# PE in source order through eight stages of a two-model kernel, with three head steps ahead of the second transposes

## The chip, the cores and the metric

The kernel runs on one core of one Trainium2 chip. The metric is the device time of one execution in microseconds; the time before is the median of three runs. The engines are called PE (TensorE, matrix products and transposes), DVE (VectorE), ACT (ScalarE), POOL (GpSimd) and SP (SyncE, which here only issues DMAs).

## The reference

256 tokens of width 1024 pass through two small models, one after the other, all in float32. What is computed, cut to the order of the parts:

```python
# first model
h = x + 0.5 * rmsnorm(swiglu(rmsnorm(h, g0), w_gu, w_down), g1)     # layer 0, FFN f00
h = h + rmsnorm(short_gated_conv(rmsnorm(h, g2)), g3)               # conv
h = h + 0.5 * rmsnorm(swiglu(rmsnorm(h, g4), ...), g5)              # FFN f01
k, v = split(rmsnorm(h, kv_norm_g) @ w_kv)                          # shared keys and values
h = h + 0.5 * rmsnorm(swiglu(rmsnorm(h, g0), ...), g1)              # layer 1, FFN f10
h = h + rmsnorm(diff_attention(rmsnorm(h, g2), k, v, ...), g3)
h = h + 0.5 * rmsnorm(swiglu(rmsnorm(h, g4), ...), g5)              # FFN f11
# second model
x = h
x = x + retention(rms_norm(x, mix_norm[0]), ...)
x = x + swiglu_2(rms_norm(x, ffn_norm[0]), ...)                     # FFN f20
x = x + stick_breaking(rms_norm(x, mix_norm[1]), ...)
x = x + swiglu_2(rms_norm(x, ffn_norm[1]), ...)                     # FFN f21
```

`swiglu` is `(silu(gate) * up) @ w_down` with a hidden width of 2816; a normed update divides the result of a stage by its root mean square before it is added to `h`.

## The kernel before

**Stages.** The kernel is a chain of stages, each a large projection from `h`, some work in the middle, and a projection back into two accumulators `acc0` and `acc1` (one for each half of 128 tokens). Stage 0 is f00, 1 conv, 2 f01, 3 the keys (`kproj`) with f10 behind them, 4 attention, 5 f11, 6 retention, 7 f20, 8 stick breaking, 9 f21. Each stage has *heads* (the first steps of its projection, for half A and for half B), a *body*, and *tails* (the steps that project back into `acc`).

**Weights.** The weights come in 280 units of 1 MB in a fixed order (`plan`). `W.load` starts the DMA of the next unit into one of three `raw` buffers; `W.split` lets ACT cast a unit into a high part `whi` (L171) and DVE subtract to get a low part `wlo` (L172), so that a product is made of three matmuls (`mm3`: L274, L275, L276; `mm_row`: L297, L300, L303). There are five slots for split units and a few spare places. `W.pump(n)` splits up to n more units as far as there is room.

**Boundary.** Between two stages, `boundary` interleaves the tails of the old stage with the heads of the new one. The tails of half A come first. `chain_A[0]` updates `h` of half A from `acc0` (squares on ACT at L386 and L388, products on DVE at L387 and L389, a power on POOL at L392, the update of `h` at L394; for a plain sum only L376 on DVE). `chain_A[1]` is eight transposes of `h` on PE (`tr_x`, L338), whose results ACT and DVE scale and split into `xT` (L321, L323); the square of `h` (L347) follows. Then come the last tail of half B, `chain_B[0]`, the first n head steps of half A, and `chain_B[1]`, the transposes of half B. A head step is twelve matmuls. In `kproj`, attention and retention the third head step also ends with four transposes of a finished column (`tr`, `tr_q`, `rotate`). Transposes write into two PSUM buffers (`ps_tr`), or, while the list `borrowed` holds a half, into that half's accumulator.

**Order on the engines.** The program is written in one sequence; a scheduling layer then picks the order of each engine's instructions by the readiness that it expects, with the source as the priority. Inside `tc.manual_schedule(engines={...})` the named engines keep the order of the source. The kernel before does that for ACT in stages 8 and 9, and for all engines in the first weight splits of the opening.

**Opening of f00.** `start` loads `x` transposed in pieces beside the first two weight units, then `h`, then the third unit. Its first two units are used by `by_tile` (48 matmuls), then come two steps of `gu(1, ...)` of 24 matmuls each, the transposes of the hidden tiles (`tr`, L520), `across` (which spreads `rstd` over the partitions by DVE at L358 and two products on PE at L359), and from column 2 on `whole` (32 matmuls each, L487 and L490). `dn` multiplies by the down projection into `acc`.

**Attention.** `s1` to `s3` make scores and their softmax, `pv1` transposes the weights of the heads (`aA`, `aB`) and copies them out, `pv2` multiplies by `v` and starts a chain over ACT, DVE and POOL (square, sum, power, product `yo` at L888), and `tr_o` transposes `yo` into the input `xk` of the projection back. In the tails `out(j, half)` is twelve matmuls.

Of the kernel before, what the change touches and what calls it, by code (L numbers as in the profile page):

```python
# [194 lines left out]
def tile_two_models(ctx: ExitStack, tc: tile.TileContext, a: dict):  # L195
# [66 lines left out]
    borrowed = []  # L262
# [139 lines left out]

    def boundary(prev_tail, chain_A, chain_B, head_A, head_B, few):
        for s in prev_tail[0]:
            s()
            W.pump(1)
        chain_A[0]()
        for s in prev_tail[1][:2]:  # L410
            s()
        chain_A[1]()
        if few:
            W.pump(1)
        for s in prev_tail[1][2:]:
            s()
        chain_B[0]()
        W.pump(1)
        n = 3 if few == 2 else 2
        for s in head_A[:n]:  # L420
            s()
        chain_B[1]()
        W.pump(1)
        for s in head_A[n:]:
            s()
            W.pump(1)
        for s in head_B:
            s()
            W.pump(1)

    def ffn(tag, xT, rstd, skew=True, first=None, last_stage=False, opening=False):
# [7 lines left out]
        def gu(c, half, j, last=True):  # L439
            if j == 0:  # L440
                gu_ps[c, half] = new_mm()
            mm_col(gu_ps[c, half], xT[half], (tag, "gu", c), j, last)
            if j == 1:
                evict(c, half)
# [69 lines left out]
        def tr(c, half):  # L514
            if c not in hT:
                hT[c] = k4.tile([P, 2, 2, 2, P], F32R, tag="k4", name=f"hT{c}")
            t = new_tr("tr_h")
            src = hid.pop((c, half))
            for k in range(2):
                T.transpose(t[:, k * P : k * P + P], src[:, k * P : k * P + P], ident)  # L520
            split_plain(t[:, 0:256].rearrange("p (k t) -> p k t", k=2), hT[c][:, half, 0], hT[c][:, half, 1])
# [22 lines left out]
        def body():  # L544
            nonlocal first
            if opening:
                for j in range(2):
                    by_tile(0, j)
                    W.pump()
                for j in range(2):  # L550
                    for half in range(2):
                        gu(1, half, j, last=half == 1)
                    W.pump()
                    for half in range(2):
                        borrowed.append(half)
                        if j == 0:
                            tr(0, half)
                        elif half == 0:
                            across(rstd)
                            acc.update(factors(rstd))  # L560
                        borrowed.pop()
            for c in range(2 if skew or opening else 0, NCH):
                for j in range(2):
                    whole(c, j)
                    borrowed.append(0)
                    if first is not None:
                        first()
                        first = None
                    if opening and c == 2 and j == 0:
                        tr(1, 0)  # L570
                        borrowed[-1] = 1
                        tr(1, 1)
                    if skew and c == 2 and j == 0:
                        tr(1, 1)
                    borrowed[-1] = 1
                    if not opening and c == (2 if skew else 0) and j == 0:
                        across(rstd)
                        acc.update(factors(rstd))
                    borrowed.pop()
                    W.pump()  # L580
                if 2 <= c < NCH - 1:
                    for half in range(2):
                        dn(c - 2, half, last=half == 1)
                    W.pump()
# [754 lines left out]
    def start(make, gcols):  # L1339
        xT, rstd = {}, {}  # L1340
        stage = make(xT, rstd)
        x_t = [k4.tile([P, 4, 2, P], F32, tag="k4", name=f"x_t{g}") for g in range(2)]

        def x_load(k, n):
            Q.dma_start(x_t[k // 4][:, k % 4 : k % 4 + n], a["x_t"][:, k : k + n])

        with tc.manual_schedule(engines={mybir.EngineType.Activation}):
            S.dma_start(gains, a["gains"])
            S.activation(small(tag="t"), nhalf[:, 0:1], AF.Silu)
        ones = junk(512)  # L1350
        V.memset(ones, 1.0)
        warm = new_acc(0, "warm")[:, 0:512]
        for _ in range(WARM):
            T.matmul(warm, ones[:, 0:P], ones, start=True, stop=True)
        W.load(4, lambda p: p % 2 or x_load(p, 2))
        x_load(4, 2)
        W.load(2, lambda p: p and x_load(6, 2))
        for half in range(2):
            Q.dma_start(h[half], x[0, half * P : half * P + P])
        W.load()  # L1360
        for half in range(2):
            xT[half] = new_xT(half)
        hi, lo = (xts[-1][:, i] for i in range(2))

        def x_in(k):
            src = x_t[k // 4][:, k % 4]
            S.activation(hi[:, k], src, AF.Copy, scale=gcols[:, k : k + 1])
            V.scalar_tensor_tensor(
                lo[:, k], src, gcols[:, k : k + 1], hi[:, k].bitcast(F32), ALU.mult, ALU.subtract
            )  # L1370

        with tc.manual_schedule():
            W.split(4, lambda p: x_in(p))
            W.split(4, lambda p: x_in(4 + p))
            for half in range(2):
                rstd[half] = rms_of(half)
        return stage

    def stage(n, make, update, gcols, prev, spares=(), gb=None, few=0, end=None):

        xT, rstd = {}, {}
        ch = xchain(update, prev[1], gcols, xT, rstd)
        heads, body, tails, acc = make(xT, rstd)
        W.spares = list(spares)
        boundary(prev[0], ch[0], ch[1], heads[0], heads[1], few)
        W.spares = []
        if end is not None:
            end()
        if gb is not None:
            gbs.append(load_gb(*gb))  # L1390
        body()
        return tails, acc
# [3 lines left out]
    def mk_ffn(tag, **kw):  # L1396
        return lambda xT, rstd: ffn(tag, xT, rstd, **kw)
# [11 lines left out]
        Q.dma_start(out[0, P : 2 * P], h[1])  # L1409

    TWO = [(0, 1), (2, 3)]
    heads, body, tails, acc = start(mk_ffn("f00", skew=False, opening=True), g_norm(0, 0))
    gbs.append(load_gb(0, 1))
    body()
# [14 lines left out]
    kT = big(2, [P, 8, 2 * P], F32, "kT")  # L1429
    heads, tr_k = kproj(xk, rstd_k, kT)  # L1430
    W.spares = [(3, 4)]
    boundary(cur[0], ch[0], ch[1], heads[0], heads[1], 0)
    W.spares = []
    gbs.append(load_gb(1, 1))
    heads, body, tails, acc = ffn("f10", xT, rstd_k, skew=False, first=lambda: tr_k(1, 1))
# [4 lines left out]
    cur = stage(5, mk_ffn("f11"), add_normed(gbs[-1], 1.0), g_norm(1, 4), cur, [(2, 3)], gb=(1, 5), few=1)  # L1440
    cur = stage(6, retention, add_normed(gbs[-1], HALF), g_cols(G_MIX, 8), cur, TWO)
    cur = stage(7, mk_ffn("f20"), add_plain, g_cols(G_FFN, 8), cur, TWO)
    act_order = tc.manual_schedule(engines={mybir.EngineType.Activation})
    act_order.__enter__()
    cur = stage(8, stick, add_plain, g_cols(G_MIX + 8, 8), cur, TWO)
# [60 lines left out]
```

## Time and profile before

| what | value |
|---|---|
| median of 3 runs (lowest to highest) | 1597.99 us (1597.76 to 1599.32) |
| the profiled execution's own time | 1596.82 us |
| span of its profile | 1595.0 us |
| PE busy | 1570.0 us, 98% |
| DVE busy | 1088.0 us, 68% |
| ACT busy | 926.8 us, 58% |
| POOL busy | 61.2 us, 4% |
| mean granted TensorE clock | 0.998 of full speed |
| DMA | 300.94 MB, 189 GB/s on average |

The span is what the profile sees from the first to the last instruction; 1.8 us of the execution lie outside it. PE is busy almost all of the time, and a busy matmul overlaps the next one, so what is lost on PE is read from the starts of its instructions.

### The profile page before, as it was taken

The page shows a single profiled execution, that of the slowest core. Times are in us where ns is not written, and L with a number is a line of the kernel's source. Part 1 is how long each engine was busy: PE and PEld are TensorE (multiplying, and loading weights), DVE is VectorE, ACT ScalarE, POOL GpSimd, SP SyncE. Part 2 cuts the span into 40 slices and gives each one's busy share as a digit, 9 for nine tenths or more (in the row PEclk, how much of TensorE's full clock was granted, in tenths as well). Part 3 has the DMA queues.
Part 4 walks back from the last instruction along what each step waited for, and adds up shares of the span by engine and source line. Part 5 has one row for each costly group of instructions (what it writes and reads, how often), then busy time and mean ns, then how long its engine had stood idle before and what let it go on. Part 6 is the DMA issues. An engine that isn't in the chain of part 4 may idle for free.

```text
span 1595.0 us, 21678 instructions
## 1 busy us (share of the span) xinstructions
PE 1570.0 (98%) x8395; PEld 1374.9 (86%) x8395; DVE 1088.0 (68%) x1742; ACT 926.8 (58%) x1611; POOL 61.2 (4%) x65
## 2 busy tenths in 40 slices
PE   8999999999999999989999999999999999999998
PEld 6899888899989999877899888888899988688997
DVE  6766867666677666787666776456567666666664
ACT  6655656555676555676555554556455566655552
POOL 0000100000000000001000010000000021000000
PEclk9999999999999999999999999999999999999999
DMA  8655644555545555444455555545455553235551
GB/s 331 238 211 189 247 159 175 204 203 197 211 175 205 205 196 213 148 159 163 176 202 209 203 196 185 185 158 188 164 206 203 205 205 138 101 134 210 211 193 46
DMA packets 43448, 300.94 MB, mean 189 GB/s; under 512 B 4864, under 2 KB 4992, under 8 KB 8016
## 3 DMA queue, kind: packets, MB, share of 16 engines
q1 hardware_dynamic: 42768, 297.81, 51.6%
q0 software_dynamic: 432, 1.64, 0.3%
q8 instruction: 66, 1.08, 0.3%
q14 instruction: 38, 0.31, 0.1%
q10 hardware_dynamic: 144, 0.09, 0.0%
HBM read 298.48 MB, written 1.05 MB: 188 GB/s over the span
## 4 chain that ended last, share of the span: by engine, by line
PE 86%; DVE 6%; ACT 4%; issue 1%; POOL 1%; DMA 1%; ACTq 0%; POOLq 0%
PE mm L487 24%; PE mm L490 12%; PE acc L303 8%; PE acc L297 8%; PE acc L300 8%; PE mm L276 7%; PE mm L274 7%; PE mm L275 7%; DVE wlo L172 2%; ACT whi L171 1%; PE tr L632 1%; POOL r L392 1%; PE tr_x L338 1%; DMA raw<-in_w 1%; PE z L1246 1%
## 5 line engine op out<-in xcount | busy, mean ns | idle before, releaser
L172 DVE TENSOR_TENSOR wlo<-raw,whi 128x1024 fp32r<-128x1024 f32 (+1 forms) x536 | 636.1, 1214 | 319.4 <-ACT whi L171 318.7
L171 ACT CAST whi<-raw 128x1024 fp32r<-128x1024 f32 (+1 forms) x536 | 540.4, 1045 | 332.3 <-issue 134.3
L487 PE MATMUL mm<-xT,whi 128*128 128x512 f32 x1792 | 584.0, 382 | 0.0
L490 PE MATMUL mm<-xT,wlo 128*128 128x256 f32 x1792 | 453.2, 273 | 0.0
L487 PEld LDWEIGHTS mm<-xT,whi 128*128 128x128 f32 x1792 | 326.3, 190 | 36.5
L490 PEld LDWEIGHTS mm<-xT,wlo 128*128 128x128 f32 x1792 | 342.7, 191 | 11.8
L274 PE MATMUL mm<-whi,xT 128*128 128x512 f32 x488 | 191.1, 392 | 2.0 <-ACT whi L171 1.4
L275 PE MATMUL mm<-wlo,xT 128*128 128x512 f32 x488 | 185.6, 380 | 0.7 <-DVE wlo L172 0.6
L276 PE MATMUL mm<-whi,xT 128*128 128x512 f32 x488 | 185.5, 380 | 0.0
L297 PE MATMUL acc<-whi,hT 128*128 128x512 f32 x516 | 153.9, 380 | 0.0
L303 PE MATMUL acc<-whi,hT 128*128 128x512 f32 x516 | 153.8, 379 | 0.0
L300 PE MATMUL acc<-wlo,hT 128*128 128x512 f32 x516 | 153.5, 379 | 0.0
L300 PEld LDWEIGHTS acc<-wlo,hT 128*128 128x128 f32 x516 | 97.5, 189 | 13.9
L303 PEld LDWEIGHTS acc<-whi,hT 128*128 128x128 f32 x516 | 97.5, 189 | 13.8
L297 PEld LDWEIGHTS acc<-whi,hT 128*128 128x128 f32 x516 | 97.3, 189 | 12.3 <-DVE hT L330 0.2
L274 PEld LDWEIGHTS mm<-whi,xT 128*128 128x128 f32 x488 | 92.1, 189 | 17.8 <-issue 2.3
L275 PEld LDWEIGHTS mm<-wlo,xT 128*128 128x128 f32 x488 | 92.3, 189 | 14.8 <-DVE wlo L172 2.3
L276 PEld LDWEIGHTS mm<-whi,xT 128*128 128x128 f32 x488 | 92.2, 189 | 14.2 <-DVE xT L323 1.2
L503 ACT COPY part<-mm 128x256 f32<-128x256 f32 x112 | 41.5, 371 | 55.6 <-PE mm L487 55.6
L329 ACT CAST hT<-hid 128x256 fp32r<-128x256 f32 x112 | 45.4, 405 | 26.1 <-DVE hid L511 26.1
L511 DVE TENSOR_TENSOR hid<-gated,sg 128x256 f32<-128x256 f32 x112 | 47.6, 425 | 11.8 <-ACT sg L507 3.7
L508 ACT COPY part<-mm 128x256 f32<-128x256 f32 x112 | 41.7, 372 | 19.1 <-PE mm L487 19.1
(246 smaller groups left out, 1622.6 us busy)
## 6 DMA issues: line engine op xcount, KB each, us to landing
raw<-in_w SPq DMA_DIRECT2D x276, 1024.0 KB, 4.8
gb<-in_norm_g SPq DMA_DIRECT2D x6, 512.0 KB, 5.6
x_t<-in_x_t SPq DMA_DIRECT2D x4, 256.0 KB, 5.5
raw<-in_w SPq DMA_DIRECT2D x4, 256.0 KB, 4.6
raw<-in_w SPq DMA_DIRECT2D x2, 512.0 KB, 7.0
h<-in_x SPq DMA_DIRECT2D x2, 512.0 KB, 8.4
dec<-in_decay POOLq DMA_DIRECT2D x1, 768.0 KB, 9.3
out<-h SPq DMA_DIRECT2D x1, 512.0 KB, 4.6
```

The source lines that it names most:

```text
L171: self.nc.scalar.copy(hi[:, c], raw[:, c])
L172: self.nc.vector.tensor_tensor(lo[:, c], raw[:, c], hi[:, c].bitcast(F32), ALU.subtract)
L274: T.matmul(o, xh, wh, start=start, stop=False)
L275: T.matmul(o, xh, wl, start=False, stop=False)
L276: T.matmul(o, xl, wh, start=False, stop=stop)
L297: T.matmul(acc[:, n * 512 : n * 512 + 512], xh(kts + k), columns(wh, c), start=st, stop=False)
L300: T.matmul(acc[:, n * 512 : n * 512 + 512], xh(kts + k), columns(wl, c), start=False, stop=False)
L303: T.matmul(acc[:, n * 512 : n * 512 + 512], xl(kts + k), columns(wh, c), start=False, stop=sp[n])
L329: S.copy(hi, tr)
L487: T.matmul(ps[n], wh[:, w], x2, start=kk == 0, stop=kk == 7, skip_group_check=True)
L490: T.matmul(o, wl[:, w], x2[:, 0], start=False, stop=False, skip_group_check=True)
L511: V.tensor_tensor(hd, t[1], sg, ALU.mult)
```

## The change

The order of PE is fixed to the source from the opening to the end of the body of stage 7. `boundary` takes the number of head steps of half A that run ahead of half B's transposes as an argument: three for a normed update (before, three only at the boundary into attention and two elsewhere), two for a plain one. In the opening, the third weight unit is loaded ahead of `h` and split in the manually ordered region ahead of the squares of `h`; the transposes of the hidden tile of column 0 follow the second step of column 1, one behind each half; `across` moves behind the first `whole` of column 2; the two transposes of column 1 follow the two `whole` steps of column 2, one each, both into `acc0`.

```diff
-    def boundary(prev_tail, chain_A, chain_B, head_A, head_B, few):
+    def boundary(prev_tail, chain_A, chain_B, head_A, head_B, few, ahead):
...
-        n = 3 if few == 2 else 2
-        for s in head_A[:n]:
+        for s in head_A[:ahead]:
             s()
         chain_B[1]()
         W.pump(1)
-        for s in head_A[n:]:
+        for s in head_A[ahead:]:
...
                         gu(1, half, j, last=half == 1)
+                        if j == 1:
+                            borrowed.append(half)
+                            tr(0, half)
+                            borrowed.pop()
                     W.pump()
-                    for half in range(2):
-                        borrowed.append(half)
-                        if j == 0:
-                            tr(0, half)
-                        elif half == 0:
-                            across(rstd)
-                            acc.update(factors(rstd))
-                        borrowed.pop()
...
-                    if opening and c == 2 and j == 0:
-                        tr(1, 0)
-                        borrowed[-1] = 1
-                        tr(1, 1)
+                    if opening and c == 2:
+                        tr(1, j)
...
-                    if not opening and c == (2 if skew else 0) and j == 0:
+                    if c == (2 if skew or opening else 0) and j == 0:
                         across(rstd)
...
+        W.load()
         for half in range(2):
             Q.dma_start(h[half], x[0, half * P : half * P + P])
-        W.load()
...
             W.split(4, lambda p: x_in(4 + p))
+            W.split()
             for half in range(2):
                 rstd[half] = rms_of(half)
...
-        boundary(prev[0], ch[0], ch[1], heads[0], heads[1], few)
+        boundary(prev[0], ch[0], ch[1], heads[0], heads[1], few, 2 if update is add_plain else 3)
...
+    pe_order = tc.manual_schedule(engines={mybir.EngineType.PE})
+    pe_order.__enter__()
     heads, body, tails, acc = start(mk_ffn("f00", skew=False, opening=True), g_norm(0, 0))
...
-    boundary(cur[0], ch[0], ch[1], heads[0], heads[1], 0)
+    boundary(cur[0], ch[0], ch[1], heads[0], heads[1], 0, 3)
...
     cur = stage(7, mk_ffn("f20"), add_plain, g_cols(G_FFN, 8), cur, TWO)
+    pe_order.__exit__(None, None, None)
```

## Rows read from the trace of the kernel before

**Rows 1.** The page's busy times: engine, busy us, share, instructions.

```profile
PE 1570.0 (98%) x8395; PEld 1374.9 (86%) x8395; DVE 1088.0 (68%) x1742; ACT 926.8 (58%) x1611; POOL 61.2 (4%) x65
```

**Rows 2.** PE's timeline in the opening: start, us, instruction, [idle before <-releaser].

```profile
17.04 0.38 PE L276 MATMUL mm<-whi,xT 128*128 128x512 f32 x1
...
20.42 0.70 PE L274 MATMUL mm<-whi,xT 128*128 128x512 f32 x2 [1.41 <-ACT whi L171]
...
22.00 0.38 PE L276 MATMUL mm<-whi,xT 128*128 128x512 f32 x1
22.22 0.38 PE L274 MATMUL mm<-whi,xT 128*128 128x512 f32 x1
```

**Rows 3.** DMA in the opening: SP's timeline, landing of issues 5 to 8 us, a window.

```profile
7.84 7.87 SPq L149 DMA_DIRECT2D raw<-in_w  x3
...
raw<-in_w SPq DMA_DIRECT2D x1, 1024.0 KB, 10.1
...
8.00:14.00 6.00, 5.97 (x27) 4.53 (x26) 4.51 (x9) 5.00 (x11) 0.00 (x0) 1.00 1.04 411
```

**Rows 4.** ACT's and DVE's timelines in the opening.

```profile
18.40 0.37 ACT L329 CAST hT<-tr_h 128x256 fp32r<-128x256 f32 x1 [0.34 <-PE tr_h L520]
...
19.32 5.79 ACT L171 CAST whi<-raw 128x1024 fp32r<-128x1024 f32 x6
...
18.80 0.42 DVE L330 TENSOR_TENSOR hT<-tr_h,hT 128x256 fp32r<-128x256 f32 x1 [0.29 <-ACT hT L329]
...
40.29 0.23 DVE L358 COPY spread<-rstd 128x128 f32<-128x128 f32 x1 [0.77 <-PE tr_r L359]
```

**Rows 5.** Windows, head matmuls alone: stretch, its us, PE busy (count), clock, DMA.

```profile
185.10:193.90 8.80, 7.32 (x32) 1.00 0.69 248
275.10:283.00 7.90, 6.64 (x30) 1.00 0.84 293
452.20:463.10 10.90, 9.64 (x43) 1.00 0.66 231
746.50:752.50 6.00, 5.34 (x24) 1.00 0.70 258
924.30:932.50 8.20, 7.87 (x34) 1.00 0.58 182
651.10:662.30 11.20, 8.82 (x38) 1.00 0.76 260
```

**Rows 6.** Windows, matmuls into the accumulators alone, same columns.

```profile
906.10:922.30 16.20, 15.49 (x71) 1.00 0.71 255
732.90:738.10 5.20, 4.35 (x19) 1.00 0.00 0
```

**Rows 7.** PE's timeline at transposes that wait, boundaries and attention.

```profile
662.36 0.66 PE L338 MATMUL tr_x<-ident,h 128*128 128x128 f32 x4 [1.29 <-ACT qT L798]
...
708.89 1.09 PE L632 MATMUL tr<-ident,yo 128*128 128x128 f32 x4 [3.54 <-DVE r L883]
...
724.17 0.70 PE L297 MATMUL acc<-whi,xk 128*128 128x512 f32 x2 [1.05 <-ACT xk L897]
...
738.17 0.66 PE L632 MATMUL tr<-ident,yo 128*128 128x128 f32 x4 [0.92 <-DVE yo L888]
...
922.34 1.29 PE L338 MATMUL tr_x<-ident,h 128*128 128x128 f32 x8 [0.66 <-DVE h L394]
...
924.40 0.48 PE L274 MATMUL mm<-whi,xT 128*128 128x512 f32 x1 [0.56 <-ACT xT L321]
```

**Rows 8.** A window behind the longest wait: all engines' busy times, then clock, DMA.

```profile
708.90:712.20 3.30, 3.30 (x11) 2.85 (x12) 1.87 (x6) 1.99 (x8) 0.00 (x0) 0.50 0.38 161
```

**Rows 9.** POOL's and DVE's timelines at the first boundary.

```profile
179.97 0.55 POOL L392 TENSOR_TENSOR r<-t,nhalf 128x1 f32<-128x1 f32 x1 [162.42 <-DVE t L391]
...
191.62 1.46 POOL L392 TENSOR_TENSOR r<-t,nhalf 128x1 f32<-128x1 f32 x1 [5.77 <-DVE t L391]
...
191.45 1.22 DVE L172 TENSOR_TENSOR wlo<-raw,whi 128x1024 fp32r<-128x1024 f32 x1
```

## The prediction

> **What bounds the kernel now.** I read the page's busy times first: PE is busy for 98% of the span, DVE for 68%, ACT for 58% [rows 1]. So PE sets the end, and a change that adds and removes no matmul can only move the time in which PE stands still. It stands for 1595.0 - 1570.0 = 25 us. Next I read PE's waits and then its timeline at each of them. Behind one another, matmuls of 512 columns start every 0.22 us (22.00 to 22.22 [rows 2]); larger steps are nearly all in a few places: the opening, the `tr_x` of each boundary, and attention. In between, the timeline shows PE already in the order of the source: steps and transposes in the bodies of conv, the FFNs and retention stand as they are written. There fixing the order changes nothing. What is left is a list of places where the trace departs from the source, and three edits. I went through them one at a time; each is worth at most a few microseconds.
>
> **Opening.** PE's first 48 matmuls are through 0.22 after 17.04 and the next 48 start at 20.42, with four transposes in between (the eight at 922.34 take 1.29 [rows 7], so some 0.5): 2.7 us. The fourth of the new ones starts at 22.00 instead of 0.65 after the first [rows 2]: 0.9 more, 0.1 of it a change of shape. So 3.5 us go, waiting for the third unit's cast and subtraction. That unit's DMA is issued at 7.84 behind `h` and lands 10.1 us later, at 17.9, while 411 GB/s flow [rows 3]. The change puts it ahead of `h`: 1 MB at that rate is 2.5 us, so it lands near 15.4 and `h` as much later. Before, its cast only began at 19.32, at 1.0 a half [rows 4]; now it follows the landing, and the subtraction (1.2, as the one in [rows 9]) follows the cast. The first half is split by 17.6, the second by 18.9; PE loses some 0.5. The squares of `h` move behind it on ACT, and with them `rstd` and the first evictions; what waits for those are the transposes of column 0, now behind 36 more matmuls (7.8 us), which cover it. The fourth unit comes behind the same bytes as before and is wanted 3 us earlier; I put 0.3 us there. On SP only the two issues of `h` stand behind the moved load; the sixth unit's load, whose buffer the earlier split frees, goes out sooner. Saved: 3.5 - 0.8 = 2.7 us.
>
> Against that stand two new waits. `across` now follows the transposes of column 1 directly. Its first spread takes a buffer of `hid`, of which there are two, both held by column 1 until a transpose frees one; the second spread takes the same one after the first product. A spread starts 0.77 us after DVE's last work, released by the product before it, and takes 0.23 [rows 4]; before, `whole` matmuls filled that time, now PE stands through it twice: 0.7 to 1.2 us each, as DVE may be in a subtraction of 1.2. And `dn(0)` starts on `acc0` right behind the last transpose, which wrote there: its copy on ACT (0.37 after 0.34) and subtraction on DVE (0.42 after 0.29) must end first, 1.4 us less PE's own 0.2, or 2 if column 2's gating is ahead on those engines [rows 4]. I take 1.7 and 1.5. Opening: 2.7 - 3.2 = 0.5 us lost (2.7 gained if another order hides both waits, 1.7 lost at worst).
>
> **Three steps ahead.** At a normed boundary PE waits for `h` of half B. The windows give the head matmuls that PE already ran ahead, and the idle time [rows 5]: 32 matmuls and 1.5 us into conv, 30 and 1.3 into f01, 24 and 0.6 into f11. Three steps are 36 matmuls: 4, 6 and 12 more, or 0.9, 1.3 and 2.6 us of cover. Gain: 0.9 + 1.2 + 0.6 = 2.7 us. No weight is late: the spare places hold the third step's unit before the old tails end.
> Into the keys the order went the other way: 43 matmuls ran and PE still lost 1.3 us [rows 5]. Seven fewer are 1.5 us less cover, the four transposes that now precede give back 0.5, the changes of shape take 0.1: 1.1 us more is idle. Into retention 34 ran with 0.3 idle, so two more would do; but its third step ends with the transposes of `rotate`, which take one of two PSUM buffers, so the second half of `tr_x` waits until DVE has read it. The same form is there into attention: `tr_x` waited 1.29 us for the copy `qT` [rows 7]. So 0.6 lost, between 0.3 gained and 1.3 lost.
>
> **Work that had been pulled forward.** In source order a waiting instruction on PE holds back all behind it; where the trace shows matmuls ahead of a wait, they now come after it.
> - Into retention, 71 matmuls into the accumulators precede half A's `tr_x` [rows 6]; the source has 60. The 11 are 2.4 us of extra waiting before 922.34; the last of them then cover the wait of 0.56 before 924.40 [rows 7] and its surroundings. Lost: 1.0 (0.4 to 2.4).
> - Into attention, two of 38 matmuls stood between the halves of `tr_x` [rows 5]: 0.6 lost with the change of shape.
> - `tr_o(0, 0)` waited until 708.89 for a chain over ACT, POOL and DVE [rows 7]; seven matmuls before it fall behind: 1.5.
> - `pv1(0, 1)` is two groups of transposes, and the second waits for a buffer; six matmuls filled that time. By the 1.29 above 1.3 at most; 0.7 taken, and 0.3 for the same at `tr_o(0, 1)`.
> - `tr_o(1, 1)` waited until 738.17 although 19 matmuls ran ahead [rows 6, 7]; the source has 12. Seven are 1.5; after them the boundary's transposes no longer wait, so 1.0.
> - `across` in f01, f11 and f20: one matmul stood between its products, 0.1 to 0.2 each: 0.4.
> Some of this comes back in attention: the wait of 1.05 at 724.17 [rows 7] is for ACT, which does not run later when PE does; I credit 1.0.
>
> Sum: 0.5 - 2.7 + 1.1 + 0.6 + 1.0 + 0.6 + 1.5 + 1.0 + 1.0 + 0.4 - 1.0 = 4.0 us longer. The profiled execution took 1596.82 us, so 1600.8; it lies 1.2 below the median, and on the median's scale that is 1598.0 + 4.0 = 1602.0 us.
>
> **Rivals.** A measurement of this kernel tells 0.2% (3.2 us) from no change: above 1601.2 is slower, below 1594.8 faster.
> *The other queues are laid out anew.* ACT, DVE and POOL keep their freedom, and the scheduling layer now orders them around a fixed PE. What delays `h` at a boundary is often a split: POOL's power took 0.55 us alone and 1.46 beside a `wlo` [rows 9]. If the new layout keeps splits out of these chains and puts the evictions of the opening first, the new waits vanish, while the two gains stay. Then 2.7 + 2.7 - 1.1 (the keys) = 4.3 us, about 1593.7; it decides for faster once more than 7 of the 8 us of new waits are hidden. For it: 0.9 us lies in every such chain. Against it: the chains into attention's `tr_o` are long whatever stands between.
> The Trainium skill (SBUF — State Buffer, "SBUF: two separate sides") says that a DVE instruction with two SBUF inputs and a GpSimd one that reads SBUF lock a shared port against each other. By it the 0.9 us is that lock, and a layout that parts the two gives it back at each boundary; the trace agrees, with 1.46 against 0.55.
> *Gains and losses cancel.* If the pulled-forward matmuls cover the next wait, as a wait put off often does, attention and retention lose 1 us instead of 5: about 1598. That the order is nearly the source's already speaks for it.
> *The clock falls again.* After the 3.54 us wait in attention TensorE was granted 0.50 of full speed, 1.2 GHz, for the window of 3.3 us that follows [rows 7, 8], so about 1.7 us of work was lost; after the shorter waits the trace shows 2.4 GHz. Half A's wait into retention grows to 0.66 + 2.4 = 3.1 us. If that is enough, and the bounds above lean the bad way, the time is 1602 + 1.7 + 2.3 = 1606.
> The Trainium skill (TensorE: Matmul & The Clock Gate, "HAM oscillation — how this bites in real kernels") says that long waits in a matmul stream put the array back on its lower clock, at each of them anew. By that rule the wait into retention adds its 1.7 to the forecast by itself, 1603.7; the trace agrees at its one wait of such length.
>
> **How the numbers follow.** My forecast, new waits larger than the two gains, has 0.53 (its own range 1599 to 1606); the re-laid queues 0.27; cancelling 0.12; the clock 0.08. Of the forecast's 0.53, 0.39 lie above 1601.2 and 0.14 within; of the re-laid queues 0.26 below 1594.8. So faster 0.26, within 0.27, slower 0.47. The range runs from the rival at 1593.7, less 1.2 for keys that also lose their wait, to 1608: the opening's worst (1.2 more), retention's (1.4 and 0.7), a second clock fall (1.7) and 1 in attention. 1592.5 to 1608 leaves out 2 in 10.
>
> **What would show it.** Right: the second 48 matmuls begin by 18; two idle stretches near `across` and before the first `dn`; 36 matmuls ahead of each normed `tr_x` and less than 0.8 us idle into conv, f01 and f11, but over 2 into the keys; `tr_o(0, 0)` idle for about 5 us. Wrong would be a third unit that is split no earlier, since the opening's gain hangs on it; ACT or DVE queues in an order in which `h` of half B comes a microsecond earlier at every boundary; or a wait elsewhere in a body, which the trace of before can't show.

## The result, and the profile after

The changed kernel takes 1615.72 us (median of 4 runs, 1614.24 to 1617.55), against 1598.65 us for the kernel before in the same runs: the ratio is 1.0107, with a 95% interval of 1.0090 to 1.0125. It is slower, as forecast, but by 17 us instead of 4, and it lies outside the predicted range. The profiled execution took 1614.69 us, with a span of 1612.9 us at a mean granted clock of 0.995.

The page's busy times, beside [rows 1]:

```profile
PE 1575.3 (98%) x8395; PEld 1379.7 (86%) x8395; DVE 1088.9 (68%) x1742; ACT 927.8 (58%) x1611; POOL 63.0 (4%) x65
```

The work is the same in number, and PE's busy time has grown by only 5.3 us. The other 12.6 us of the longer span (1612.9 - 1595.0 = 17.9) are time in which PE stands still. PE's waits in the changed kernel (total, times, longest) say where:

```profile
PE tr_x L338 <- DVE h L394: 7.2, 4, 4.1
PE tr L626 <- DVE r L877: 5.0, 1, 5.0
PE tr_r L359 <- DVE spread L358: 3.9, 5, 2.3
PE acc L297 <- ACT whi L171: 2.7, 1, 2.7
PE tr L626 <- DVE yo L882: 2.4, 1, 2.4
```

To see where the time was lost, follow one mark through the three traces: the start of the first `whole` matmul (L487) of each FFN. The third column is experiment E1 below, the changed kernel with PE's order left free. The second row is the 129th matmul of L487 and L490 in f00, behind the opening's transposes and the first products of `dn`.

| start of | before | changed | changed, PE free | changed - before | PE free - before |
|---|---|---|---|---|---|
| f00 | 31.72 | 28.93 | 28.19 | -2.79 | -3.53 |
| f00, 129th | 64.12 | 71.44 | 60.40 | +7.32 | -3.72 |
| f01 | 299.01 | 306.91 | 294.61 | +7.90 | -4.40 |
| f10 | 477.18 | 486.23 | 472.49 | +9.05 | -4.69 |
| f11 | 769.38 | 782.16 | 764.10 | +12.78 | -5.28 |
| f20 | 1137.65 | 1155.52 | 1131.92 | +17.87 | -5.73 |
| f21 | 1438.34 | 1456.30 | 1432.56 | +17.96 | -5.78 |

The changed kernel is 2.8 us ahead when f00 begins, loses 10.1 in the opening right behind that, 0.6 up to f01, 1.2 at the keys, 3.7 in attention and 5.1 into retention, and nothing from f20 on: the order is still fixed through f20's body, and free behind it.

**Opening.** The third unit came as early as forecast. The second 48 matmuls follow the first without the gap of [rows 2]. PE's timeline of the changed kernel (the last of the first 48, then the first two of the second):

```profile
17.50 0.38 PE L276 MATMUL mm<-whi,xT 128*128 128x512 f32 x1
17.72 0.38 PE L274 MATMUL mm<-whi,xT 128*128 128x512 f32 x1
18.04 0.48 PE L275 MATMUL mm<-wlo,xT 128*128 128x512 f32 x1
```

Then PE stands three times, first at the two products of `across` and later at the first product of `dn`. Its timeline, and under it DVE's and ACT's:

```profile
34.25 0.38 PE L520 MATMUL tr_h<-ident,hid 128*128 128x128 f32 x2
35.78 0.46 PE L359 MATMUL tr_r<-ident,spread 128*128 128x128 f32 x2 [1.15 <-DVE spread L358]
38.57 0.49 PE L359 MATMUL tr_r<-ident,spread 128*128 128x128 f32 x2 [2.33 <-DVE spread L358]
...
45.80 0.38 PE L520 MATMUL tr_h<-ident,hid 128*128 128x128 f32 x2
48.84 0.67 PE L297 MATMUL acc<-whi,hT 128*128 128x512 f32 x2 [2.65 <-ACT whi L171]
```

```profile
35.42 0.22 DVE L358 COPY spread<-rstd 128x128 f32<-128x128 f32 x1
36.02 2.36 DVE L172 TENSOR_TENSOR wlo<-raw,whi 128x1024 fp32r<-128x1024 f32 x2 [0.39 <-ACT whi L171]
38.30 0.22 DVE L358 COPY spread<-rstd 128x128 f32<-128x128 f32 x1
...
46.18 0.42 DVE L511 TENSOR_TENSOR hid<-gated,sg 128x256 f32<-128x256 f32 x1
46.52 0.42 DVE L504 TENSOR_TENSOR gated<-mm,part 128x256 f32<-128x256 f32 x1
46.85 0.41 DVE L509 TENSOR_TENSOR gated<-mm,part 128x256 f32<-128x256 f32 x1
47.18 0.42 DVE L505 TENSOR_TENSOR gated<-gated,rows 128x256 f32<-128x256 f32 x1
47.93 0.42 DVE L330 TENSOR_TENSOR hT<-hid,hT 128x256 fp32r<-128x256 f32 x1 [0.33 <-ACT hT L329]
48.27 0.42 DVE L330 TENSOR_TENSOR hT<-tr_h,hT 128x256 fp32r<-128x256 f32 x1
```

```profile
46.27 0.38 ACT L329 CAST hT<-tr_h 128x256 fp32r<-128x256 f32 x1
46.54 1.06 ACT L171 CAST whi<-raw 128x1024 fp32r<-128x1024 f32 x1
```

The second spread needs the `hid` buffer that the first product frees, just after 35.78. In DVE's queue two weight subtractions (2.36 us) stand ahead of it, and PE, with its order fixed, has nothing else that it may run. At `dn` the profile names the cast `whi`, but the work that ends last before 48.84 is DVE's subtraction `hT<-tr_h` at 48.27: five DVE operations of column 2's gating stand ahead of it (E3 below shows that it is `acc0` that `dn` waits for). A wait for several semaphores is put down to one of them, and here the timeline of the other engines corrects it.

**The clock.** Windows of the changed kernel (stretch, length, busy times, granted clock, DMA share, GB/s), behind the waits at `across` and at `dn` and behind the two long ones of attention and retention:

```profile
39.50:42.80 3.30, 3.30 (x13) 2.81 (x12) 2.55 (x5) 1.32 (x2) 0.00 (x0) 0.51 0.83 333
...
49.80:53.10 3.30, 3.30 (x9) 2.61 (x8) 1.83 (x4) 0.41 (x1) 0.00 (x0) 0.51 0.32 127
...
719.10:722.10 3.00, 3.00 (x9) 2.46 (x8) 1.98 (x6) 1.17 (x5) 0.00 (x0) 0.50 0.10 41
...
937.30:940.60 3.30, 3.30 (x11) 2.76 (x10) 2.89 (x11) 3.18 (x11) 0.00 (x0) 0.50 0.62 243
```

The kernel before had one such stretch in these stages, the one in attention [rows 8]. Three are new, 3.3 us each at half of full speed, so 3 × 3.3 × 0.5 = 5 us of the 17.9. They count as busy time, which is where PE's extra 5.3 us of it come from.

**Attention and retention.** PE's timeline at the transposes of [rows 7]:

```profile
718.32 1.09 PE L626 MATMUL tr<-ident,yo 128*128 128x128 f32 x4 [5.03 <-DVE r L877]
...
750.84 0.66 PE L626 MATMUL tr<-ident,yo 128*128 128x128 f32 x4 [2.43 <-DVE yo L882]
...
936.38 1.53 PE L338 MATMUL tr_x<-ident,h 128*128 128x128 f32 x8 [4.08 <-DVE h L394]
...
951.89 0.63 PE L338 MATMUL tr_x<-ident,h 128*128 128x128 f32 x4 [1.30 <-DVE ts L1032]
```

These are the waits that were forecast, at the places that were forecast: 3.54 became 5.03, 0.92 became 2.43, 0.66 became 4.08, and the wait for `rotate`'s buffer (L1032) is new. Into retention the chain that updates `h` was also late. On ACT a weight cast stands ahead of the second square of `acc0`; it stands there in the kernel before too, but here it first waited for its data:

```profile
930.81 1.04 ACT L171 CAST whi<-raw 128x1024 fp32r<-128x1024 f32 x1 [2.96 <-DMA raw<-in_w]
931.76 0.59 ACT L388 ACTIVATE junk<-acc 128x512 bf16<-128x512 f32 x1
```

In E3 and E11 below the wait ahead of these transposes is 3.02 us; in E11's trace that cast waits for no data. So about 1.1 of the 4.08 goes with the late cast, and the rest with the order.

### The profile page after: what moved, and what is told of

The parts are those of the page before. It is cut to its first block, busy times and chain, and to the rows that moved or that the text cites. A ratio compares the mean times of both kernels' runs of the same rounds, so it can differ in the third digit from the quotient of the medians.

```text
span 1612.9 us, 21680 instructions
## 1 busy us (share of the span) xinstructions
PE 1575.3 (98%) x8395; PEld 1379.7 (86%) x8395; DVE 1088.9 (68%) x1742; ACT 927.8 (58%) x1611; POOL 63.0 (4%) x65
## 3 DMA queue, kind: packets, MB, share of 16 engines
HBM read 298.48 MB, written 1.05 MB: 186 GB/s over the span
## 4 chain that ended last, share of the span: by engine, by line
PE 86%; DVE 6%; ACT 4%; issue 2%; POOL 1%; DMA 1%; SPq 0%; ACTq 0%; POOLq 0%; DVEq 0%
PE mm L487 24%; PE mm L490 12%; PE acc L297 8%; PE acc L303 8%; PE acc L300 8%; PE mm L274 7%; PE mm L275 7%; PE mm L276 7%; DVE wlo L172 2%; ACT whi L171 1%; DMA raw<-in_w 1%; PE tr L626 1%; ACT s L825 1%; POOL r L392 1%; PE tr_x L338 1%
## 5 line engine op out<-in xcount | busy, mean ns | idle before, releaser
L487 PE MATMUL mm<-xT,whi 128*128 128x512 f32 x1792 | 585.2, 383 | 0.0
L490 PE MATMUL mm<-xT,wlo 128*128 128x256 f32 x1792 | 453.7, 274 | 0.0
L487 PEld LDWEIGHTS mm<-xT,whi 128*128 128x128 f32 x1792 | 327.1, 190 | 36.8
L490 PEld LDWEIGHTS mm<-xT,wlo 128*128 128x128 f32 x1792 | 343.5, 192 | 11.8
```

The lines of the kernel that those rows point to most:

```text
L487: T.matmul(ps[n], wh[:, w], x2, start=kk == 0, stop=kk == 7, skip_group_check=True)
L490: T.matmul(o, wl[:, w], x2[:, 0], start=False, stop=False, skip_group_check=True)
```

## The experiments

Theory: the change is a gain of some 7 us (the early unit and the third step) and a loss of some 25 us that comes from fixing PE's order, place by place, wherever the source asks PE to wait while other matmuls are ready. Rivals: the loss comes from the other edits (the moved `across`, the bank of the transposes); or fixing the order costs everywhere, in the bodies too; or the later losses are only the opening's lateness passed on. Ratios are to the kernel before on the same chip, which took medians of 1598.2 to 1598.6 us in these runs.

**E1: the change without the pin.**

```diff
-    pe_order = tc.manual_schedule(engines={mybir.EngineType.PE})
-    pe_order.__enter__()
...
-    pe_order.__exit__(None, None, None)
```

> The changed kernel with PE's order left to the scheduling layer; the opening's new order, the earlier third unit and the third head step stay. If the fixed order is what costs (theory), PE moves other work into the waits again and the time is 1594 to 1600 us: the earlier unit gives back about 2.8. If the cost lies in the rearranged opening or the third head step themselves (rival), it stays above 1608.

Measured: 1591.03 us, ratio 0.9951 (0.9937 to 0.9966), 3 us below the range that was expected. With nothing taken away but the fixed order, the change is faster than the kernel before and than the changed one. The pin alone costs 1615.72 - 1591.03 = 24.7 us. PE's timeline in the opening shows what the free order does (15 matmuls stand between the two products, 14 of them left out here):

```profile
35.62 0.38 PE L359 MATMUL tr_r<-ident,spread 128*128 128x128 f32 x2
35.76 0.36 PE L490 MATMUL mm<-xT,wlo 128*128 128x256 f32 x1
...
38.24 0.39 PE L359 MATMUL tr_r<-ident,spread 128*128 128x128 f32 x2
```

The second product comes 2.6 us behind the first, as in the pinned kernel (2.8), but matmuls of `whole` fill that time. And PE's waits, the ones that answer to the list above:

```profile
PE tr L626 <- DVE r L877: 3.8, 1, 3.8
PE tr_x L338 <- DVE h L394: 2.6, 4, 1.3
...
PE tr L626 <- DVE yo L882: 0.9, 1, 0.9
```

**E2: the pin alone, from behind f00's body to stage 7, on the kernel before.** The kernel before has two steps ahead at most boundaries. The pin starts behind the opening, because the old opening's spread needs a buffer that only transposes later in the source set free.

```diff
     body()
+    pe_order = tc.manual_schedule(engines={mybir.EngineType.PE})
+    pe_order.__enter__()
     cur = tails, acc
...
+    pe_order.__exit__(None, None, None)
```

> The kernel before, with PE's order fixed from behind the body of f00 to the end of stage 7; opening as before, two head steps ahead. Theory: of the 17.9 us lost, 10.6 lie behind the opening although three steps help at conv, f01 and f11; with two steps the pulled-forward matmuls are lost too, so 1610 to 1614 us. Rival (the loss is the opening's, and what follows is drift of the weights' transfers): 1598 to 1602.

Measured: 1623.9 us, ratio 1.0153 (1.0138 to 1.0168). That is a miss: it was expected to be faster than the changed kernel, and it is slower although its opening is free. PE's wait for `h` at the boundaries reads:

```profile
PE tr_x L338 <- DVE h L394: 17.0, 7, 5.4
```

against 7.2 with three steps. So the third step is worth some 10 us of waiting when PE's order is fixed. With PE free it is worth much less (E6), because the free order already runs matmuls past the waiting transposes. Not all of E2's loss is the pin's: its trace has seven stretches at a granted clock of 0.50 up to f20, where the kernel before has one, and the first (21.0 to 27.6) lies in the opening, which is not pinned; f00 starts 3.4 us later there than in the kernel before.

**E3 and E4: the opening's waits, with the pin kept.** E3 lets the last transposes of column 1 use both accumulators in turn, so that `dn`'s first product doesn't follow the copy of the very last one. E4 does that too and writes the spread into a buffer of its own.

```diff
                     if opening and c == 2:
+                        borrowed[-1] = j
                         tr(1, j)
```

```diff
-            d = wk.tile([P, 256], F32, tag="hid", name="spread")[:, 0:P]
+            d = rows[:, half * P : half * P + P]
```

> The changed kernel with the last transposes of the opening written to acc1 instead of acc0, so that the first down projection, which starts on acc0, need not wait for them. Theory: the wait of 2.8 us and the fall of TensorE's clock behind it (1.7 us) go, 1611 us. Rival (the wait is for hT of column 0 or for the engines' backlog, not for acc0): within 1.5 us of 1615.7.

> As the one before, and the spreads of across are written into the rows buffer instead of one of the two hid buffers. Theory: the spreads are ready before PE asks, so the two waits of 1.3 and 2.5 us and the clock's fall behind them (1.7) go as well: the opening then keeps its gain and the time is 1605 to 1607 us. Rival (DVE's backlog of subtractions holds the spreads, not the buffer): 1609 to 1612.

Measured: E3 1609.63 us, ratio 1.0071 (1.0054 to 1.0088); E4 1607.83 us, ratio 1.0056 (1.0037 to 1.0074). In E3 the wait at `dn` is gone, and the time fell by 6.1 us by the medians, 4.6 by the spans of the profiled executions (1608.3 against 1612.9); the wait of 2.65 and the 1.65 of half clock behind it would be 4.3 of that. Up to the 129th matmul of f00, E3 is only 3.2 us ahead (68.24 against 71.44), because in its execution the half clock behind `across` lasts longer, until 44.4 instead of 42.9; the other 1.4 came behind the opening. In E4 the waits at `across` are gone, but `dn`'s first product into the other accumulator waits instead (a window of E3, then PE's timeline of E4):

```profile
38.50:44.30 5.80, 5.80 (x19) 5.07 (x20) 4.12 (x5) 2.23 (x4) 0.00 (x0) 0.50 0.84 298
```

```profile
45.59 1.12 PE L297 MATMUL acc<-whi,hT 128*128 128x512 f32 x2 [2.84 <-DVE hT L330]
```

So E4 gains little over E3 (1.8 us, while its four runs lie 6.3 us apart), and it falls between its two ranges, 1 us above the theory's and 1 us below the rival's. In its trace splits of weights stand in DVE's queue ahead of the subtraction that `dn` now waits for, so the rival is right in part: the buffer held the spreads, and the backlog holds what comes next. Mending the two named causes brings back 7.9 us together. The 16.8 us left over E1 are this new wait, the clock, and what lies behind the opening.

**E5 and E6: each of the other edits alone, on the kernel before, PE free.**

```diff
+        W.load()
         for half in range(2):
             Q.dma_start(h[half], x[0, half * P : half * P + P])
-        W.load()
...
+            W.split()
             for half in range(2):
                 rstd[half] = rms_of(half)
```

```diff
...
-        boundary(prev[0], ch[0], ch[1], heads[0], heads[1], few)
+        boundary(prev[0], ch[0], ch[1], heads[0], heads[1], few, 2 if update is add_plain else 3)
...
-    boundary(cur[0], ch[0], ch[1], heads[0], heads[1], 0)
+    boundary(cur[0], ch[0], ch[1], heads[0], heads[1], 0, 3)
```

> The kernel before, with the third weight unit loaded ahead of h and split ahead of the opening's row statistics; PE free, nothing else changed. The opening's first whole tile started 2.8 us sooner in the changed kernel and 3.5 us sooner in it without the pin. Theory (this edit is worth what the prediction said, and nothing behind it gives it back while PE is free): 1598.65 - 3.6 = about 1595. Rival (the opening's other waits give it back, as in the pinned kernel): 1598 to 1599.

> The kernel before, with three steps ahead of the transposes at boundaries with a normed update; PE free, nothing else changed. Theory (the third step covers the waits ahead of conv and f01 and costs nothing elsewhere): about 1596.5, 2 us less than before. Rival (where PE is free its order is chosen by due times anyway, so that the third step changes nothing): 1598.3 to 1599.

Measured: E5 1593.44 us, ratio 0.9973 (0.9962 to 0.9983). E6 1594.21 us, ratio 0.9981 (0.9973 to 0.9990). Each is a gain of its own, 4.8 and 4.0 us by the medians, and 8.8 together, beside the 7.2 of E1; by the ratios 4.3 and 3.0, 7.3 together, beside 7.8, with intervals of about 1.5 us to either side. The trace of E5 agrees: its f00 starts at 28.14, 3.6 us sooner. The trace of E6 can't carry its gain, since that execution took 1597.33, 3.1 above the median of its runs; from its f00 to its f21 it is 0.8 us shorter than the kernel before. Its opening, which is that of the kernel before, shows why: behind the waits of 1.41 and 0.56 for the third unit [rows 2] the clock fell in this execution, where it didn't in the trace of the kernel before, and f00 starts 1.4 us later (windows of E6, then of the kernel before):

```profile
21.20:24.60 3.40, 2.94 (x7) 2.40 (x8) 3.40 (x4) 3.40 (x5) 0.00 (x0) 0.51 0.73 249
```

```profile
21.20:24.60 3.40, 2.92 (x14) 2.57 (x15) 3.40 (x4) 3.40 (x5) 0.00 (x0) 1.00 0.78 295
```

The early unit takes these waits away, which may be why E5 gains more by its runs than the 3.6 us of its trace; that was not tried by itself. From E5 to E1, the stretch from f00 to f21 is 2.9 us shorter, and that difference holds the order of the opening as well. So the third step with PE free is worth between 0.8 and 4.0 us.

**E7: the pin in the bodies only.** PE's order is fixed in the bodies of conv, f01, f10, f11, retention and f20, and free in the opening, the boundaries and attention.

```diff
...
-        body()
+        if n in (1, 2, 5, 6, 7):
+            with tc.manual_schedule(engines={mybir.EngineType.PE}):
+                body()
+        else:
+            body()
...
```

> The changed kernel with PE's order written out only in the bodies of conv, f01, f10, f11, retention and f20; the opening, the boundaries and attention are left free. Theory (the pin costs where another order than the source's is better: the opening, the boundaries, attention; in the bodies the source's order is what the free queue has anyway): 1591 to 1593, as without the pin. Rival (the pin costs in the bodies too): over 1596.

Measured: 1591.88 us, ratio 0.9963 (0.9950 to 0.9976), as without the pin. Over these long stretches fixing the order costs nothing that the runs can tell, and gains nothing either.

**E9, E10, E11: the pin in one place each.** Each is the changed kernel without its pin, and with the order fixed around the opening and f00's body (E9), around stages 4 and 5, which is attention and the boundary behind it (E10), or around stages 6 and 7, which is retention, its boundaries and f20 (E11).

```diff
+    with tc.manual_schedule(engines={mybir.EngineType.PE}):
+        heads, body, tails, acc = start(mk_ffn("f00", skew=False, opening=True), g_norm(0, 0))
+        gbs.append(load_gb(0, 1))
+        body()
...
```

> The changed kernel with PE's order written out in the opening alone (from the first instruction to the end of f00's body), PE free behind it. By the two traces, changed kernel against the one without the pin, the pin costs 7.3 + 3.7 = 11.0 us up to the second half of f00. Theory (each stage's loss stands by itself): 1591.0 + 11.0 = 1602. Rival (what is lost in the opening is made up behind it where PE is free, or what is lost behind it hangs on the opening's lateness): under 1598.

> The changed kernel with PE's order written out in attention's stage and in the boundary behind it alone. By the two traces the pin costs 3.7 + 0.6 = 4.3 us between the first matmuls of f10 and those of f11. Theory (each stage's loss stands by itself): 1591.0 + 4.3 = 1595.3. Rival (attention has its wait at the same transposes without the pin, 4.0 against 5.2 us, so that the pin there costs no more than 1.5): 1591.5 to 1592.5.

> The changed kernel with PE's order written out in retention's stage, its boundaries included, and in f20 alone. By the two traces the pin costs 5.1 + 0.4 = 5.5 us between the first matmuls of f11 and those of f20, a fall of the clock at retention's boundary included. Theory (the boundary's wait comes from retention's own order): 1596.5. Rival (the chain at that boundary is late because of what was lost ahead of it; with PE free ahead of it the wait stays near 0.8): 1591 to 1593.

Measured: E9 1602.55 us, ratio 1.0024 (1.0014 to 1.0033); E10 1597.28 us, ratio 0.9994 (0.9983 to 1.0005); E11 1595.78 us, ratio 0.9977 (0.9968 to 0.9987). Over E1's 1591.03 that is 11.5, 6.3 and 4.8 us, 22.5 together. Conv, f01 and the keys were not pinned alone; by the table they hold another (7.90 + 4.40) - (7.32 + 3.72) = 1.26 and (9.05 + 4.69) - (7.90 + 4.40) = 1.44. With these the sum is 25.2, against 24.7 for the whole pin; the runs of E9, E10 and E11 lie 4 to 6 us apart, so that so close an agreement is partly chance. So the losses add up place by place within that spread, and the rival that the later ones hang on the opening falls. E10 came out 2 us above its 4.3: in its trace f11 starts 5.7 us later than in E1, but 1.5 of these are lost before f01, where nothing is pinned, and 4.2 from there to f11. Those 1.5 are no cost of the pin: 1.04 of them is a wait for half A into conv, which the trace of E12 has as well (0.99), where PE is free throughout. The waits of E10 and of E11, in that order:

```profile
706.31 1.09 PE L626 MATMUL tr<-ident,yo 128*128 128x128 f32 x4 [5.31 <-DVE r L877]
```

```profile
917.95 1.65 PE L338 MATMUL tr_x<-ident,h 128*128 128x128 f32 x8 [3.02 <-DVE h L394]
```

They are there with PE free in all of the kernel ahead of them.

**E8 and E12: attempts at a better version, PE free.** E8 takes E1 and moves `tr_o(0, 0)` in attention's body behind `s1(3, 1)`, where its chain would have had more time. E12 takes E1 with four steps ahead at the keys and at attention.

```diff
             pv1(1, 0)
-            tr_o(0, 0)
             vp(3, 1, 1)
             W.pump(1)
             pv2(1, 0)
             s1(3, 1)
+            tr_o(0, 0)
```

```diff
...
-        boundary(prev[0], ch[0], ch[1], heads[0], heads[1], few, 2 if update is add_plain else 3)
+        boundary(prev[0], ch[0], ch[1], heads[0], heads[1], few, 4 if few == 2 else 2 if update is add_plain else 3)
...
-    boundary(cur[0], ch[0], ch[1], heads[0], heads[1], 0, 3)
+    boundary(cur[0], ch[0], ch[1], heads[0], heads[1], 0, 4)
```

> The changed kernel without the pin, and with the transposes of attention's first output half moved behind the second pair's scores in the source. Theory (the wait of 4.0 us at them is the softmax's chain, which one more block of matmuls ahead of it covers, and the half clock behind that wait goes with it): 1591.0 - 4.0 - 1.7 + 1 for what the output's own copies are late by = about 1586.5. Rival (the wait moves to the output's first matmul, which waits for the copies of the same transposes): 1590.5 to 1592.

> The changed kernel without the pin, and with four steps instead of three ahead of the transposes at the boundaries of keys and attention, where waits of 1.43 and 1.45 us are left. Theory (a fourth step covers these waits): 1591.0 - 2.9 + 0.5 = about 1588.5. Rival (with PE free the queue has put its steps where its costs say, and what the fourth step covers comes back at the second half's transposes): 1590.5 to 1592.

Measured: E8 1594.91 us, ratio 0.9982 (0.9973 to 0.9991), a miss for the theory, and above the rival's range too; E12 1591.47 us, ratio 0.9955 (0.9941 to 0.9970), as its rival said. In E8 the wait moved to the matmuls that use the transposes:

```profile
704.23 0.66 PE L626 MATMUL tr<-ident,yo 128*128 128x128 f32 x4 [0.66 <-DVE yo L882]
709.27 1.22 PE L297 MATMUL acc<-whi,xk 128*128 128x512 f32 x2 [4.38 <-ACT xk L891]
```

The two waits are 5.0 us together, where E1 waits 3.8 at the transposes and 1.0 at `acc`: the transposes are free sooner, but nothing independent is left behind them. The loss comes behind them: two more waits of 0.41 and 0.73 follow, and the granted clock stays at 0.50 until 717.4, with 7.0 us of busy time at half speed, where E1 has 3.5 and is back at full speed from 708.1 on. That is 0.2 + 1.1 + 1.7 = 3.0 us, and from f10 to f11 the trace of E8 is 3.1 longer than that of E1 (294.7 against 291.6). A window of E8:

```profile
709.30:717.40 8.10, 6.96 (x20) 5.21 (x21) 7.57 (x13) 4.82 (x12) 0.91 (x1) 0.50 0.21 62
```

The fastest version run is E1, the change without its pin; E12 can't be told from it.

## Why the prediction was off

**What held.** PE sets the end, and a change that leaves its work as it is can only move the time in which it stands still. The early unit was put at 2.7 us and gave 2.8 (3.6 in E5). Fixing the order changes nothing in the bodies (E7). The waits listed as signs came: two idle stretches at `across`, one at `dn`, over 2 us into the keys (2.36 for `h`), about 5 at `tr_o(0, 0)` (5.03), less than 0.8 into conv (0.55 for half B), f01 and f11. Single sizes held well: `tr_o(0, 0)` and `tr_o(1, 1)` were put at 1.5 more each, and wait 1.49 and 1.51 more. The keys were put at 1.1 and lost 1.2. The terms from f10 to f11 added up to 0.6 + 1.5 + 1.0 + 1.0 - 1.0 - 0.6 = 2.5 us, and 3.7 were lost; the difference is about the credit of 1.0, which did not come: the wait of 1.05 at `acc` [rows 7], from which it was drawn, is still 0.9.

**What failed: the prices of two places, and the clock behind them.**

1. "Against that stand two new waits ... I take 1.7 and 1.5." They are 1.15 + 2.33 = 3.5 and 2.65. For each I had priced only the operations of the chain itself, and those at the lower end of the time that DVE may be in other work. What set the wait was the other work in DVE's queue: two subtractions of 1.2 us ahead of the second spread, five gating operations ahead of the subtraction that `dn` waits for. The bound "1.7 lost at worst" for the opening took this as one subtraction; the opening lost 7.3.
2. No fall of the clock was counted in the opening. Two stretches of 3.3 us at half speed followed, which cost 1.65 each, 3.3 us together. The rival of the falling clock was put at retention alone, where it came true: it said 3.1 us of waiting, the wait was 4.08 (3.02 where the cast was not late), 3.4 more than before [rows 7], and the clock fell. With the 1.65 behind it and the 1.30 at `rotate`'s buffer this makes 6.4 us; some 0.8 of waits that stood there before are gone, and 5.1 us were lost, where the sum had 1.0 + 0.6 = 1.6. What the sum had wrong there: it took back 1.4 of the 2.4 us of extra waiting, put 0.6 for the wait at `rotate`, and had nothing for a late cast (1.1) and for the clock (1.65). "No weight is late" was asked of the matmuls alone; ACT's queue waited 2.96 us for one.
3. "Three steps ahead ... Gain: 0.9 + 1.2 + 0.6" came at the waits that it was worked out from, and yet did not show in the time. The waits for half B, 1.42 into conv and 1.16 into f01 before, are 0.55 and none, 2.0 us of the 2.1 forecast for these two. But from the 129th matmul of f00 to f01 the changed kernel lost 0.6 us. One part is a new wait of 1.05 for half A of conv: on DVE, three subtractions of units that are split into spare places (`sp`, 3.49 us at once) stand ahead of the products that update `h`. They stand there in the kernel before too, but end 1.3 us earlier against the squares. That wait is not the pin's: E6 has it as well (1.04), with PE free. Small waits make another 0.6, and the last 1.0 lies in no wait and was not traced.

DVE's timeline into conv, and under it PE's wait for half B there, changed kernel:

```profile
183.19 3.49 DVE L172 TENSOR_TENSOR sp<-raw,sp 128x1024 fp32r<-128x1024 f32 x3
186.60 0.68 DVE L387 TENSOR_TENSOR y<-acc,gb 128x512 f32<-128x512 f32 x1
```

```profile
202.94 1.32 PE L338 MATMUL tr_x<-ident,h 128*128 128x128 f32 x8 [0.55 <-DVE h L394]
```

Point 1, the wait in point 3 and the late cast ahead of retention are one mistake: each wait was costed as a chain alone, and on the path that sets the end the chain stood in queues that serve the weight splits as well. The rival "the other queues are laid out anew" looked at this, but with the wrong sign: it let the new layout take splits out of the chains, and at the opening, conv and retention they stood in them.

The Trainium skill (TensorE: Matmul & The Clock Gate, "Step-by-step: what each phase is for") states that matmuls stay in program order, and that only weight loads are pulled ahead. The trace agrees: in the 4.3 us between 34.25 and 38.57 the pinned kernel's PE runs nothing but transposes and the first product, and in E1 matmuls stand between them only because the program has them there. The same page of the Trainium skill ("HAM oscillation — how this bites in real kernels") says that long waits in a matmul stream bring the lower clock back at each of them. The traces of the changed kernel agree for the waits of 4.08 and 5.03 us. By that rule the fall into retention belonged in the forecast with its wait, as the prediction said; of the shorter waits of the opening the rule, which speaks of long ones, says nothing, and the last section shows both outcomes at waits of up to 3.5 us.

## What to carry to other kernels

Writing out an engine's order costs nothing where it is the order that a free queue has anyway, and at each other place it costs the whole wait, since everything behind it waits too: look for the places where the trace departs from the source, leave those free (pinning the rest gained nothing here), and price a wait by the queue that its producer stands in, with all its other work ahead, not by the producer's own chain. Test bundled edits apart from each other: here two that gain 3 to 5 us each were hidden under a third that loses 25.

## What the runs showed of the hardware

After a wait of the same length the clock fell in one execution and not in another. The wait for `h` into retention took 3.02 us in E3 and in E11. In E11 the granted clock behind it was 0.50, in E3 it was 1.00 (windows of E11, then of E3):

```profile
919.80:922.00 2.20, 2.20 (x7) 1.73 (x6) 2.20 (x10) 2.02 (x6) 0.00 (x0) 0.50 0.39 164
```

```profile
934.60:936.50 1.90, 1.90 (x11) 1.69 (x10) 1.71 (x6) 1.90 (x8) 0.00 (x0) 1.00 0.84 354
467.90:471.00 3.10, 3.10 (x9) 2.47 (x8) 2.37 (x10) 3.10 (x11) 0.55 (x1) 0.50 0.64 240
```

The last row stands behind the 2.36 us wait into the keys in E3; behind the same 2.36 us in the changed kernel the matmuls of 512 columns follow each other every 0.22 us, at full speed. The long wait in attention is no exception: it took 3.54 us in the kernel before, where the clock fell to 0.50 [rows 7, 8], and 3.52 in E9, where it stayed at 1.00 (PE's timeline of E9, then a window):

```profile
715.43 0.63 PE L626 MATMUL tr<-ident,yo 128*128 128x128 f32 x4 [3.52 <-DVE r L877]
```

```profile
715.50:718.70 3.20, 3.20 (x23) 2.89 (x25) 1.84 (x6) 3.01 (x10) 0.00 (x0) 1.00 0.33 138
```

So the length of a wait does not decide it by itself, and a kernel with several waits of 2 to 4 us has a time that varies: four runs of E1 lie within 0.8 us of each other, four of E4 within 6.3. The mean granted clock goes with the time: of E10's ten runs, the five at 0.998 or more took 1595.5 to 1596.9 us, the four at 0.995 took 1599.2 to 1601.4. What decides whether the clock falls was not tried.
